# Per-token scales in 128 partitions: a row in DRAM and broadcast loads in place of products with diagonals

## The chip, the cores and the metric

The kernel runs on one core of a Trainium2 chip. The time is the device time of one execution in microseconds, as the median of several runs. PE is the engine for matrix products, DVE the vector engine, ACT the one for activations, POOL is GpSimd; SP issues the DMAs, all of them on one queue here, in the order of the program.

## The reference

One encoder layer, applied to a prompt of 256 tokens and a sample of 2048, width 1024, in float32:

```python
h = rms_norm(x, g_pre)
proj = h @ w_in                     # q, k, v, z_a, u_f, z_f, 512 columns each
y_a = neighbourhood_attention(q, k, v, rpb)
y_f = fourier_mix(u_f, w_fourier, b_fourier)
mixed = concat([rms_norm(y_a, g_na) * silu(z_a), rms_norm(y_f, g_f) * silu(z_f)])
out = mixed @ w_out
return x + rms_norm(out, g_post)
```

`rms_norm` multiplies each token by `rsqrt(mean(x*x) + 1e-6)` and each column by `g`. The change is about the first of these, the token's scale of `h`.

## The kernel before

**Products.** Each product in full precision is three matmuls (`mm3`, L164 to L166) on a high and a low part of both operands. The high part is a cast by ACT, the low part a difference by DVE. For most of the sample the kernel multiplies fewer blocks by forming sums and differences of blocks of `x` and of the weights first.

**Token scales.** `rows_square` sums the squares of rows with tokens on partitions, and `row_scales` makes the scales: column `c` of `invt` (128 x 18) holds those of the 128 tokens of tile `c`. Tiles 0 and 1 are the prompt, 2 to 9 the first half of the sample, 10 to 17 its second half. `row_scales` runs three times: for columns 0 to 3, 4 to 9, and much later 10 to 17.

Where a product has tokens on its output's partitions, the scale is applied afterwards, one number a partition (`vu_out`, L339, into `vo` and `uo`). Where `x` lies with its columns on partitions and tokens along the row, the scales must be a row of numbers that stands in every one of the 128 partitions. Two places need it: `xp` (L721, the prompt, then split into `ph` and `pl`) and `n_scale` (L404, tiles `nx` of the sample, on which the sums and differences are then formed; first half with `x` None, second half with `x` 0 and 1).

Before, such a row is made on PE. `diag` lets ACT multiply the identity by a column of `invt`, which gives a diagonal matrix `dg`; `spread` multiplies a matrix of ones (`onesq`) by it, so that each output partition holds the scales of 128 tokens in order (L309), in PSUM tiles `ivt` (prompt) and `iv` (two of 512 tokens a half). DVE reads them there.

**Order.** All engines follow the order of the program, written out by hand. Ahead of the place come `u` and `v` products for tiles `c` 0 to 2, then a loop over `c` = 3, 4, 5: at `c` = 3 SP issues three loads of `wz`, ACT makes ten diagonals, DVE forms sums `r_sum`; after the products of `c` = 3 PE makes the first ten spreads. At `c` = 4 DVE makes `xp`. Then 16 blocks `b` multiply `ph` and `pl` by weights, split into `wh` and `wl` two blocks ahead (`b_raw`, L566 to L571), while `n_scale` works on `nx` for the first half (`b` < 8). `vu` forms more of `u` and `v`. Then a loop over `i` of 16 and `j` of 7 multiplies the sample by the other weights: at `i` = 0 the last `row_scales` (`j` = 1), eight diagonals (`j` = 2) and eight spreads (`j` = 4) for the second half; `n_scale` for it runs at `i` = 1 and 3. Later come `vu` for the second half, the Fourier stages (`u_load`, tile `ut`), the attention and the output product.

Buffers of the tag `vw` (three of 128 x 1024) are used by `vh` in `vu` and by `ut` later; `iv` in the changed kernel takes them too.

Of the kernel before, what the change touches and what calls it, by code (L numbers as in the profile page):

```python
# [10 lines left out]
F32 = mybir.dt.float32  # L11
F32R = mybir.dt.float32r
AF = mybir.ActivationFunctionType
ALU = mybir.AluOpType
# [4 lines left out]
T = TP + TS  # L19
# [149 lines left out]
def build(tc, A, O):  # L169
    nc = tc.nc  # L170
# [3 lines left out]
    dr = es.enter_context(tc.tile_pool(name="dr", bufs=1, space=DRAM))  # L174
# [10 lines left out]
    vN, uN = [dr.tile([2, 32, 32, 512], F32, name=n) for n in ("vN", "uN")]  # L185
    sD = dr.tile([5, 128, 4, 512], F32, name="sD")
    xD = dr.tile([7, 128, 4, 512], F32, name="xD")
    oD = dr.tile([T, D], F32, name="oD")
    yD = dr.tile([2, 4, 128, T], F32, name="yD")
    woD = dr.tile([2, 2, 4, 128, D], F32, name="woD")  # L190
# [2 lines left out]
    ident = cst.tile([128, 128], F32, name="ident")  # L193
# [7 lines left out]
    invt = cst.tile([128, 18], F32, name="invt")  # L201
# [9 lines left out]
    hp = ph.enter_context(tc.tile_pool(name="hp", bufs=1))  # L211
    st = ph.enter_context(tc.tile_pool(name="st", bufs=2))
    ps = es.enter_context(tc.tile_pool(name="ps", bufs=3, space=PSUM))
# [90 lines left out]
        nc.vector.scalar_tensor_tensor(out=invt[:, c0:c0 + n], in0=t, scalar=1.5, in1=y, op0=ALU.add, op1=ALU.mult)  # L304


    def spread(p, c0, n):
        for x in range(n):
            nc.tensor.matmul(p[:, 128 * x:128 * x + 128], onesq, dg[c0][:, 128 * x:128 * x + 128], start=True, stop=True)  # L309
        dg.pop(c0)  # L310

    def diag(c0, n):
        dg[c0] = et("dg")
        for x in range(n):
            nc.scalar.activation(dg[c0][:, 128 * x:128 * x + 128], ident, AF.Copy, scale=invt[:, c0 + x:c0 + x + 1])

    ivp, dg = {}, {}

    def diag_group(sg):
        for b in range(2):  # L320
            diag(2 + 8 * sg + 4 * b, 4)

    def spread_group(sg):
        ivp[sg] = [ps.tile([128, 512], F32, tag="b", name="iv", bufs=2) for b in range(2)]
        for b in range(2):
            spread(ivp[sg][b], 2 + 8 * sg + 4 * b, 4)

    def p_mm(m, c, kps):
        if (m, c) not in acc:
# [5 lines left out]
    def vu_out(m, c):  # L335
        s, b = PL[c]
        o = st.tile([128, 512], F32, tag="f", name=m + "o", bufs=3)
        x = row_tile(c)
        nc.scalar.activation(o, acc.pop((m, c)), AF.Copy, scale=invt[:, x:x + 1])  # L339
        if s is not None:  # L340
            put_rows(m, 0, b, s, o)
        elif m == "u":
            nc.sync.dma_start(uD[c * 128:c * 128 + 128, :], o)
        else:
            for r in range(4):
                nc.sync.dma_start(vP[c, r, 8 * c:8 * c + 32], o[32 * r:32 * r + 32])
                x = 24 * (1 - c)
                nc.sync.dma_start(vP[1 - c, r, 32 * c:32 * c + 8], o[32 * r + x:32 * r + x + 8])
# [51 lines left out]
    def n_scale(x, kh, b, ks=range(4)):  # L400
        v_ = nq[kh, b] if x is None else nq[x, kh, b]
        for k in ks if x is None else range(2):
            kk = 4 * kh + 2 * (x or 0) + k
            nc.vector.scalar_tensor_tensor(out=v_[:, k], in0=v_[:, k], scalar=gpre[:, kk:kk + 1],  # L404
                                           in1=ivp[int(x is not None)][b], op0=ALU.mult, op1=ALU.mult)

    def n_put(x, j, kh, b):
        nc.sync.dma_start(xD[j, :, 2 * x:2 * x + 2], nq[x, kh, b])
# [75 lines left out]
    def et(name):  # L484
        return st.tile([128, 512], F32, tag="e", name=name, bufs=6)
# [200 lines left out]

    for c in range(3):
        vu_out("u", c)

    def wo_load(x):  # L690
        wor[x] = load((128, D), A["wo"][x // 4, x % 4], "wr")
# [11 lines left out]
    for c in range(3, 6):  # L703
        if c < 5:
            wz_load(3)
            x_split(c + 1)
        if c == 3:
            diag(0, 2)
            diag_group(0)
            for q in range(8):  # L710
                r_sum(q)
        if c == 4:
            n_load((0, 0))
            for x in range(1, 5):
                r_put(x)
            xp = k8(F32, "xp", (128, KC, 256))
            hp_, lp_ = [k8(F32R, "p" + x, (128, KC, 256)) for x in "hl"]
            for k in range(KC):
                for t in range(2):
                    ts = slice(128 * t, 128 * t + 128)  # L720
                    nc.vector.scalar_tensor_tensor(out=xp[:, k, ts], in0=xs[t][:, k], scalar=gpre[:, k:k + 1],  # L721
                                                   in1=ivt[:, ts], op0=ALU.mult, op1=ALU.mult)
            nc.scalar.copy(hp_, xp)
            nc.vector.tensor_tensor(out=lp_, in0=xp, in1=f_(hp_), op=ALU.subtract)
        if c == 5:
            n_load((1, 0))
            b_raw(0)
            b_raw(1)
        p_mm("v", c, range(4))
        vu_out("v", c)  # L730
        p_mm("u", c, range(4))
        if c == 3:
            ivt = ps.tile([128, 256], F32, tag="c", name="ivt", bufs=1)
            spread(ivt, 0, 2)
            spread_group(0)
        vu_out("u", c)


    for b in range(16):
# [11 lines left out]
        if b < 8:  # L751
            x, y = divmod(b, 2)
# [63 lines left out]
    for i in range(16):  # L816
# [48 lines left out]
        for j in range(7):  # L865
            if i in (0, 8):
                if j in (0, 3):
                    w_load(i + 1 + j // 3)
                if i == 0 and j == 0:
                    a_split(0, 6)  # L870
                if i == 0 and j == 1:
                    row_scales(10, 8)
                if i == 0 and j == 2:
                    diag_group(1)
                if i == 0 and j == 4:
                    spread_group(1)
                if j == 2:
                    w_sums(i + 1)
                for x in {3: (0, 1), 4: (2, 3), 5: (4, 5), 6: (6,)}.get(j, ()):
                    a_split(i + 1, x)  # L880
            elif i not in (7, 15):
                if j == 0:
                    w_sums(i + 1)
                a_split(i + 1, j)
                if j == 3 and i < 14 and i != 6:
                    w_load(i + 2)
            elif i == 7:
                if j in (3, 4):
                    op_load(j - 3)
                if j in (5, 6):  # L890
                    op_split(j - 5)
                if j == 5:
                    wo_load(0)
            if sg == 0:
                x, y = divmod(7 * (pr - 1) + j, 14)
                if x in (0, 1):
                    if y == 0:
                        n_load(x)
                    elif 3 <= y < 7:
                        n_scale(x, *divmod(y - 3, 2))  # L900
                    elif 7 <= y < 12:
                        n_diff(x, y - 7)
                if pr == 6 and j in (2, 5):
                    (b_split if j > 2 else b_get)(0)
                if pr == 7 and j:
                    b_get(j)
                    if j > 2:
                        b_split(j - 2)
            if i == 2 and j == 0:
                for t, n in ((gmix, "gmix"), (bfs, "bf"), (dnyq, "dnyq"), (rmask, "rmask"), (csm, "csmask")):  # L910
                    nc.sync.dma_start(t, A[n])
                nc.sync.dma_start(cm, A["cmask"].rearrange("p (b x) -> p b x", b=2))
            if i == 5 or 8 <= i < 15:
                t_step(max(0, i - 7), j)
            for f, d in ((u_load, 0), (u_split, 3), (u_stage1, 5)):
                x = 7 * pr + j - 7 - d
                if sg and 0 <= x < 36 and x % 7 in (0, 2, 4):
                    f(x // 7 * 3 + x % 7 // 2)
            if i == 15 and j in (1, 3, 4, 5):
                if j == 1:  # L920
                    d2 = [load_d(0), load_d(1)]
                else:
                    zgs.append(load_z(j - 3))
            if 9 <= i < 15 and j == 2:
                v_copy(i - 9)
            p = mmt(512)
            aw = aop[i, j]
            bh, bl = bnew[sg, j]
            for k in range(4):
                mm3(nc, p, aw[:, 0, k], aw[:, 1, k], bh[:, k], bl[:, k], k == 0, k == 3)  # L930
            add = lambda o, u: nc.vector.tensor_tensor(out=e_(o), in0=uu[u], in1=p, op=ALU.add)
            if j == 0:
                nc.scalar.copy(e_("u0"), p)
            elif j == 1:
                comb(0, 0, "u0", p)
            elif j == 2:
                add("u2", "u0")
            elif j == 3:
                add("u4", "u2")
            elif j == 4:  # L940
                comb(1, 1, "u4", p)
                add("u3", "u2")
            elif j == 5:
                comb(1, 0, "u3", p, ALU.subtract)
                store(1)
            else:
                comb(0, 1, "u4", p)
                store(0)
# [788 lines left out]
```

## Time and profile before

| | |
|---|---|
| median of 3 runs | 988.64 us (988.61 to 988.85) |
| the profiled execution | 989.52 us, its span 987.4 us |
| PE busy | 970.9 us (98%) |
| DVE, ACT, POOL busy | 703.6, 501.7, 428.3 us |
| DMA | 278.70 MB, mean 282 GB/s |
| products with diagonals (L309) | 36 records on PE, from 51.9 to 174.7 us |
| diagonals (L315) | 18 activations of 386 ns |

A row of a group of instructions has line, engine, operation and tiles (written <- read), count, shortest, median and longest duration in ns, and the first and last start in us. A row of a timeline has start and duration in us, engine, line and tiles, and in brackets the idle time of the engine before it and what ended it; several instructions in a row are merged. A row of waits has who waited for whom, the time in us, how often, and the longest. A row of a window has the stretch, its length, the busy time in it of PE, PE's weight loads, DVE, ACT and POOL, the share of full clock that PE had, the share of time in which the 16 DMA engines were busy, and GB/s.

### The profile page before, as it was taken

Reading aid. Unit: us, or ns where it says so; the run is one execution under the profiler, and the core shown is the slowest. Engines: PE = TensorE matmul, PEld = TensorE weight load, DVE = VectorE, ACT = ScalarE, POOL = GpSimd, SP = SyncE. Lnnn points to the kernel's source line nnn. Section 1 sums busy time; section 2 is a strip of 40 time slices with the busy share of each in tenths; the row PEclk is TensorE's granted clock in tenths of the full one; section 3 lists DMA queues with packets and bytes.
Section 4 is the critical chain, followed back from the end, with each engine's and each line's share of the span. In section 5 each row is a group of like instructions: output and inputs, shape, how many; then the busy total and the mean of one; then the engine's idle time right before and its main releaser. Section 6 shows DMA issues by size and latency. Waiting matters only on the chain.

```text
span 987.4 us, 17038 instructions
## 1 busy us (share of the span) xinstructions
PE 970.9 (98%) x5774; PEld 805.5 (82%) x5774; DVE 703.6 (71%) x1301; ACT 501.7 (51%) x1083; POOL 428.3 (43%) x400
## 2 busy tenths in 40 slices
PE   7999999999999999999999999999999999999997
PEld 6889988888888878878887879778787887888886
DVE  6378987777866777777976446775665665659997
ACT  6836676433224533333344255677666675644443
POOL 3100002464741102755755033566587686534444
PEclk9999999999999999999999999999999999999999
DMA  9899686566839997598989887697768799779993
GB/s 327 303 380 340 190 330 249 173 221 247 308 148 358 347 387 260 218 337 313 322 314 339 294 312 296 218 277 263 247 213 260 261 309 315 224 245 340 344 338 125
DMA packets 147046, 278.70 MB, mean 282 GB/s; under 512 B 14160, under 2 KB 85136, under 8 KB 143568
## 3 DMA queue, kind: packets, MB, share of 16 engines
q1 hardware_dynamic: 146960, 277.62, 79.9%
q8 instruction: 46, 0.75, 0.3%
q14 instruction: 40, 0.33, 0.1%
HBM read 183.19 MB, written 101.71 MB: 289 GB/s over the span
## 4 chain that ended last, share of the span: by engine, by line
PE 48%; DMA 2%; DVE 1%; issue 1%; ACT 0%; POOL 0%; SPq 0%; DVEq 0%; ACTq 0%; POOLq 0%
PE po L1406 19%; PE pv L1476 6%; PE ptb L1460 5%; PE s L1155 4%; PE mm L165 2%; PE mm L164 2%; PE mm L166 2%; PE pab L1000 2%; DMA ut<-uN 1%; PE py L164 1%; PE py L166 1%; PE py L165 1%; DMA tb<-tD 1%; DVE ut L372 0%; PE ppq L1038 0%
## 5 line engine op out<-in xcount | busy, mean ns | idle before, releaser
L164 PE MATMUL mm<-xh,wa 128*128 128x512 f32 x448 | 174.4, 389 | 0.0
L165 PE MATMUL mm<-xl,wa 128*128 128x512 f32 x448 | 174.3, 389 | 0.0
L166 PE MATMUL mm<-xh,wa 128*128 128x512 f32 x448 | 174.3, 389 | 0.0
L536 POOL TENSOR_TENSOR ws<-wr 128x512 f32<-128x512 f32 x16 | 22.5, 1408 | 238.8 <-DMA wr<-wz 223.5
L1189 POOL TENSOR_SCALAR w<-w,m 128x480 f32<-128x480 f32 (+6 forms) x136 | 83.3, 625 | 64.6 <-DVE m L1186 50.6
L165 PEld LDWEIGHTS mm<-xl,wa 128*128 128x128 f32 x448 | 84.1, 188 | 17.5
L166 PEld LDWEIGHTS mm<-xh,wa 128*128 128x128 f32 x448 | 84.1, 188 | 17.5
L164 PEld LDWEIGHTS mm<-xh,wa 128*128 128x128 f32 x448 | 84.1, 188 | 17.5
L1406 PE MATMUL po<-wo,yh 128*128 128x512 f32 x272 | 90.4, 413 | 0.0
L1182 ACT ACTIVATE w<-w,m 128x480 f32<-128x480 f32 (+6 forms) x136 | 79.2, 585 | 15.5 <-DVE m L1177 15.5
L1406 PE MATMUL po<-w,yh 128*128 128x512 f32 x280 | 86.7, 391 | 0.0
L551 DVE TENSOR_TENSOR wa<-wr,wa 128x512 fp32r<-128x512 f32 x60 | 62.3, 1045 | 32.0 <-ACT wa L550 31.9
L1177 DVE CUSTOM_DVE_ANT_1 w<-s,tb 128x360 f32<-128x360 f32 (+5 forms) x124 | 62.5, 541 | 9.1 <-PE s L1155 8.5
L165 PE MATMUL mm<-vl,xh 128*128 128x512 f32 x168 | 65.6, 390 | 0.9 <-DVE vl L482 0.9
L589 POOL TENSOR_TENSOR mt<-mt,rmask 128x880 f32<-128x880 f32 (+2 forms) x24 | 53.7, 2250 | 27.6 <-DMA ut<-uN 15.5
L166 PE MATMUL mm<-vh,xl 128*128 128x512 f32 x168 | 65.4, 389 | 0.0
L164 PE MATMUL mm<-vh,xh 128*128 128x512 f32 x168 | 65.4, 389 | 0.0
L1476 PEld LDWEIGHTS pv<-pt,v 128*64 128x64 f32 (+4 forms) x896 | 47.4, 135 | 19.0 <-issue 14.9
L1476 PE MATMUL pv<-pt,v 128*64 128x128 f32 (+4 forms) x896 | 62.3, 280 | 0.0
L854 DVE TENSOR_TENSOR f<-u,mm 128x512 f32<-128x512 f32 x64 | 43.6, 681 | 25.2 <-PE mm L166 15.4
L1406 PEld LDWEIGHTS po<-w,yh 128*128 128x128 f32 x280 | 52.3, 188 | 10.9 <-issue 0.2
L1460 PE MATMUL ptb<-ident,w 128*128 128x128 f32 (+4 forms) x428 | 59.9, 277 | 0.0
(253 smaller groups left out, 2384.9 us busy)
## 6 DMA issues: line engine op xcount, KB each, us to landing
wr<-wz SPq DMA_DIRECT2D x48, 512.0 KB
vl<-sD SPq DMA_DIRECT2D x20, 512.0 KB
xm<-xm SPq DMA_DIRECT2D x9, 1024.0 KB
oD<-ofs SPq DMA_DIRECT2D x18, 512.0 KB
of<-oD SPq DMA_DIRECT2D x18, 512.0 KB
yr<-yD SPq DMA_DIRECT2D x34, 256.0 KB
zD<-f SPq DMA_DIRECT2D x16, 512.0 KB
woD<-wo SPq DMA_DIRECT2D x16, 512.0 KB
```

The costliest lines, as they stand in the source:

```text
L164: nc.tensor.matmul(out, lh, rh, start=first, stop=False)
L165: nc.tensor.matmul(out, lh, rl, start=False, stop=False)
L166: nc.tensor.matmul(out, ll, rh, start=False, stop=last)
L551: nc.vector.tensor_tensor(out=o[:, 1], in0=src, in1=o[:, 0].bitcast(F32), op=ALU.subtract)
L589: nc.gpsimd.tensor_tensor(out=o, in0=i, in1=rmask[:, m0:m0 + n].unsqueeze(2).to_broadcast([128, n, 80]), op=ALU.add)
L854: nc.vector.tensor_tensor(out=dst(f, b), in0=src(uu[u]), in1=src(p), op=op)
L1177: nc.vector.tensor_tensor_reduce(out=rows(g["w"][b][:, h, :n], w), in0=rows(g["s"][2 * b + h][:, :n], w), in1=tv, scale=1.0, scalar=3.0e38 ...
L1182: nc.scalar.activation(w, w, AF.Exp, bias=m[:, h:h + 1], scale=-1.0, accum_out=m[:, 2 + h:3 + h])
L1189: nc.gpsimd.tensor_scalar(w, w, m[:, 4 + h:5 + h], 1.0, ALU.mult, ALU.mult)
L1406: nc.tensor.matmul(p, (d["l"] if x == 2 else d["h"])[:, c], w(n, int(x == 1), c), start=j == 0, stop=j == 11)
L1460: nc.tensor.transpose(ptb[h][:nk, j * 128:j * 128 + 128], g["w"][b][:, h, c0:c0 + nk], ident)
L1476: nc.tensor.matmul(p[hs, b], g["v"][:nk, v, hs], g["pt"][b][:nk, h, j * 128:j * 128 + 128], start=j == 0, stop=j == len(ch) - 1)
```

## The change

`diag`, `spread` and their groups go. `iv_put` stores columns of `invt` as one row of `ivD` in DRAM, and `iv_get` loads a stretch of that row into all 128 partitions, into an SBUF tile `iv`. The columns 0 to 9 are stored after the `u` outputs of `c` = 2 and loaded at `c` = 3 in two parts (prompt, first half), where the diagonals were made; columns 10 to 17 are stored at `i` = 0, `j` = 3 and loaded at `j` = 5. All of these DMAs are on SP's queue. `xp` and `n_scale` read the SBUF tile.

```diff
+    ivD = dr.tile([1, T], F32, name="ivD")
...
-    def spread(p, c0, n):
-        for x in range(n):
-            nc.tensor.matmul(p[:, 128 * x:128 * x + 128], onesq, dg[c0][:, 128 * x:128 * x + 128], start=True, stop=True)
-        dg.pop(c0)
-
-    def diag(c0, n):
-        dg[c0] = et("dg")
-        for x in range(n):
-            nc.scalar.activation(dg[c0][:, 128 * x:128 * x + 128], ident, AF.Copy, scale=invt[:, c0 + x:c0 + x + 1])
...
+    ivb = {}
+
+    def iv_put(c0, n):
+        nc.sync.dma_start(ivD[0, c0 * 128:(c0 + n) * 128].rearrange("(c p) -> p c", p=128), invt[:, c0:c0 + n])
+
+    def iv_get(c0, n):
+        t = hp.tile([128, 1024], F32, tag="vw", name="iv", bufs=3)
+        nc.sync.dma_start(t[:, :128 * n], ivD[:, c0 * 128:(c0 + n) * 128].to_broadcast([128, 128 * n]))
+        ivb[c0] = t
...
-                                           in1=ivp[int(x is not None)][b], op0=ALU.mult, op1=ALU.mult)
+                                           in1=ivb[2 if x is None else 10][:, 512 * b:512 * b + 512], op0=ALU.mult, op1=ALU.mult)
...
     for c in range(3):
         vu_out("u", c)
+    iv_put(0, 10)
...
         if c == 3:
-            diag(0, 2)
-            diag_group(0)
+            iv_get(0, 2)
+            iv_get(2, 8)
...
-                                                   in1=ivt[:, ts], op0=ALU.mult, op1=ALU.mult)
+                                                   in1=ivb[0][:, ts], op0=ALU.mult, op1=ALU.mult)
...
-        if c == 3:
-            ivt = ps.tile([128, 256], F32, tag="c", name="ivt", bufs=1)
-            spread(ivt, 0, 2)
-            spread_group(0)
...
-                if i == 0 and j == 2:
-                    diag_group(1)
-                if i == 0 and j == 4:
-                    spread_group(1)
+                if i == 0 and j == 3:
+                    iv_put(10, 8)
+                if i == 0 and j == 5:
+                    iv_get(10, 8)
```

More of the change, by code (lines that the diff above doesn't have):

```diff
@@ L304, in row_scales @@
         nc.vector.scalar_tensor_tensor(out=invt[:, c0:c0 + n], in0=t, scalar=1.5, in1=y, op0=ALU.add, op1=ALU.mult)
-    def spread(p, c0, n):
-        for x in range(n):
-            nc.tensor.matmul(p[:, 128 * x:128 * x + 128], onesq, dg[c0][:, 128 * x:128 * x + 128], start=True, stop=True)
-        dg.pop(c0)
-    def diag(c0, n):
-        dg[c0] = et("dg")
-        for x in range(n):
[L315 to L326, printed above, removed]
+    ivb = {}
[5 more added lines that the diff above has]
+        ivb[c0] = t
     def p_mm(m, c, kps):
```

## The prediction, made before the changed kernel ran

> **What bounds the kernel now.** I read the page first, then who waited for whom on PE, then the instructions on the two tiles that the change removes, and last the timelines around them.
>
> ```profile
> PE 970.9 (98%) x5774; PEld 805.5 (82%) x5774; DVE 703.6 (71%) x1301; ACT 501.7 (51%) x1083; POOL 428.3 (43%) x400
> ...
> q1 hardware_dynamic: 146960, 277.62, 79.9%
> ...
> PE 48%; DMA 2%; DVE 1%; issue 1%; ACT 0%; POOL 0%; SPq 0%; DVEq 0%; ACTq 0%; POOLq 0%
> ```
>
> PE is busy for 98% of the span, and where the chain of the work that ended last leaves PE, it does so for a few per cent only. Busy time of pipelined matmuls can flatter, so I checked what PE waited for:
>
> ```profile
> PE mm L164 <- ACT xh L283: 5.4, 1, 5.4
> PE pz L165 <- DVE ut L372: 1.5, 2, 0.9
> PE mm L165 <- DVE vl L482: 0.9, 2, 0.7
> PE mm L166 <- DVE wl L570: 0.6, 3, 0.2
> ```
>
> The first is PE's first wait, at the start of the kernel. All the others together are about 3 us of 987. So an instruction that leaves PE's queue is worth its whole slot, unless a stretch in which something else sets the pace swallows it; and the change can cost time only by making PE wait. These two questions carry the rest.
>
> **What leaves PE.**
>
> ```profile
> L309 PE MATMUL iv<-dg,onesq x32: 270/275/275, 52.4 to 174.7; 128*128 128x128 f32 x32
> L315 ACT ACTIVATE dg<-ident,invt x18: 386/387/402, 48.4 to 171.5; 128x128 f32<-128x128 f32 x18
> ...
> L309 PE MATMUL ivt<-dg,onesq x4: 270/274/275, 51.9 to 52.3; 128*128 128x128 f32 x4
> ```
>
> Eighteen products with a diagonal show as 36 records, two each, in two places: 20 near 52 us and 16 near 173 us. Their durations overlap, so 36 times 275 ns would be far too much. What counts is the start of the next ordinary matmul:
>
> ```profile
> 51.70 0.39 PE L166 MATMUL mm<-wc,xl 128*128 128x512 f32 x1
> 51.93 0.60 PE L309 MATMUL ivt<-dg,onesq 128*128 128x128 f32 x4
> 52.37 1.95 PE L309 MATMUL iv<-dg,onesq 128*128 128x128 f32 x16
> ...
> 54.39 0.40 PE L165 MATMUL mm<-wc,xh 128*128 128x512 f32 x1
> ```
>
> ```profile
> 172.78 0.39 PE L166 MATMUL mm<-xh,wa 128*128 128x512 f32 x1
> 173.01 1.95 PE L309 MATMUL iv<-dg,onesq 128*128 128x128 f32 x16
> ...
> 175.02 0.40 PE L165 MATMUL mm<-xl,wa 128*128 128x512 f32 x1
> ```
>
> From one ordinary matmul to the next is 51.93 - 51.70 = 0.23 us (0.227 over longer rows). From the L166 at 51.70 to the second ordinary one after the products, at 54.39, are 2.69 us, where two pitches are 0.455: 2.24 us go. I take the second because the first is itself stretched. At 173 us: 175.02 - 172.78 = 2.24, less 0.455, is 1.79 us. Sum 4.03 us, 0.112 us a record.
>
> On ACT 18 activations of 0.387 us go. ACT is busy half of the time and no PE wait in this part is on it, so I count nothing for that. No PSUM tile is waited for here either, so the freed banks count nothing.
>
> **What comes in, first place.** One store writes 10 columns of 128 scales as one row, then two loads bring 128 KB and 512 KB into 128 partitions. All are on SP's queue: the store behind the store of `uo` for c=2, the loads behind the next three loads of `wz`. SP stands at the first load until the store has landed; behind it are the stores of `vo` and `uo` for c=3 and three more `wz` loads.
>
> ```profile
> 47.55 0.32 SPq L352 DMA_DIRECT2D uN<-uo  x1
> 47.96 1.34 SPq L231 DMA_DIRECT2D wr<-wz  x3
> ...
> 51.99 0.33 SPq L352 DMA_DIRECT2D vN<-vo  x1
> ...
> 53.34 2.21 SPq L231 DMA_DIRECT2D wr<-wz  x3
> ```
>
> The store goes out at about 47.9 us. The scales are ready by then, since the activations into `uo` read them. No transfer of the trace has 4-byte runs, so its time is unknown. The nearest row for its fixed part is the load of `gpre`, 128 runs of 32 B:
>
> ```profile
> 1.18 0.42 SPq L624 DMA_DIRECT2D gpre<-gpre  x1
> ...
> 4.21 0.72 ACT L253 ACTIVATE wc<-rv,gpre 128x512 fp32r<-128x512 f32 x1 [1.99 <-DMA gpre<-gpre]
> ```
>
> That took 3.0 us from issue to use. The store has 1280 runs, 80 on each of 16 engines, instead of 8: 72 more. Each costs between nothing and a mean packet: 79.9% of 16 x 987.4 us over 146,960 packets is 86 ns, for 1.9 KB. So the store lands between 47.9 + 3.0 = 50.9 and 50.9 + 72 x 0.086 = 57.1 us. I take 52, near the low end, as the runs carry 4 B and not 1.9 KB. SP had nothing to issue from 49.3 to 51.99 anyway, so at 52 the stores behind slip by a microsecond; at 57 they and the `wz` loads slip by about 5.
>
> The loads then take about the 3 us of `gpre`'s from issue to use, the second behind the first. So the scales of the prompt are there at 55, at worst at 60.1. Who needs them, and when?
>
> ```profile
> 59.85 4.21 DVE L721 SCALAR_TENSOR_TENSOR xp<-xr,gpre,ivt 128x128 f32<-128x128 f32 x16
> ...
> 68.25 2.35 DVE L567 TENSOR_TENSOR wl<-wr,wh 128x1024 fp32r<-128x1024 f32 x2
> 77.84 1.23 DVE L567 TENSOR_TENSOR wl<-wr,wh 128x1024 fp32r<-128x1024 f32 x1 [7.23 <-ACT wh L566]
> ```
>
> ```profile
> 75.93 0.28 PE L164 MATMUL mm<-ph,wh 128*128 128x256 f32 x1
> ```
>
> DVE comes to `xp` at 59.85 because it is busy until then, and the first `wl` behind it ends at about 69.4 (68.25 and half of 2.35), 9.6 us after `xp` begins. PE needs both at 75.93, after the change at 73.7. So `xp` may begin as late as 64.1 before PE waits: even the worst store leaves 4 us. After that DVE stood for 7.23 us, released by ACT and behind it PE, so that stretch moves forward with PE.
>
> The 0.64 MB come while the DMA engines are full (below), at about 400 GB/s, so what is queued behind lands 1.6 us later: inside the slack just worked out, and DVE's idle 7 us.
>
> ```profile
> 50.00:52.00 2.00, 2.00 (x11) 1.65 (x10) 2.00 (x3) 1.96 (x6) 0.00 (x0) 1.00 1.01 387
> ```
>
> **Second place.** The scales are made at 169.2 and first read at 192.5:
>
> ```profile
> 169.20 0.17 DVE L304 SCALAR_TENSOR_TENSOR invt<-rt,ry 128x8 f32<-128x8 f32 x1
> ...
> 192.53 1.40 DVE L404 SCALAR_TENSOR_TENSOR nx<-nx,gpre,iv 128x512 f32<-128x512 f32 x2
> ```
>
> ```profile
> 167.24 1.79 SPq L231 DMA_DIRECT2D wr<-wz  x4
> 183.54 3.63 SPq L860 DMA_DIRECT2D zD<-f  x2
> ```
>
> ```profile
> 175.00:180.00 5.00, 5.00 (x23) 4.13 (x22) 3.76 (x5) 2.25 (x4) 3.88 (x3) 1.00 0.00 0
> ```
>
> The store queues behind four `wz` loads that are through by 175 (the DMA engines then stand still), lands by about 177, at worst 6.2 us later, 183, and the load is there 3 us after it, at 186. SP has nothing to issue until 183.54. `n_scale` comes 1.79 us earlier than before against all this, at 190.7, so nothing is late; a store 4.7 us slower than my worst would make DVE wait.
>
> **DVE's operand.** `xp` and `n_scale` read the scales from SBUF instead of PSUM. The same operation with all operands in SBUF, L254, took as long:
>
> ```profile
> L404 DVE SCALAR_TENSOR_TENSOR nx<-nx,gpre,iv x32: 732/742/746, 79.0 to 242.7; 128x512 f32<-128x512 f32 x32
> ```
>
> ```profile
> L254 DVE SCALAR_TENSOR_TENSOR wc<-rv,gpre,wc x8: 745/751/753, 5.0 to 15.8; 128x512 fp32r<-128x512 f32 x8
> ```
>
> Nothing for that; where GpSimd works beside it, after 192 us, it may be slower, on an engine that is not the bound there.
>
> **Sum.** 2.24 + 1.79 = 4.03 us, costs 0. The profiled execution took 989.52 us, its span 987.4 and 2.1 around it; it would become 985.5. It lies 0.9 over the median of the runs, 988.64, so the runs should show 988.64 - 4.03 = 984.6 us.
>
> **Rivals.** *The store's 4-byte runs are slow, and the kernel becomes slower.* Place: `xp` at 59.85, by way of SP standing behind the store. PE begins to wait when the store lands after 61 us, 13.2 us after its issue, so at (13.2 - 3.0) / 72 = 142 ns a run; it has lost the 4.03 us at 198 ns. At 250 ns the store takes 3.0 + 18.0 = 21.0 us, 7.8 beyond the start of the waiting, and the time is 988.64 - 4.03 + 7.8 = 992.4 (the second place adds a wait of DVE, which I leave out). For it: all 1280 runs go into the same 5 KB of DRAM, from all engines at once, and no row has such a store. Against it: it takes three times the mean packet for a five-hundredth of its bytes.
>
> The Trainium skill's "DMA: Bandwidth & Descriptors" speaks for this rival in "Rules for kernel authors" (a strided last dimension becomes one descriptor per element) and in "Specifications" (transfers under 512 B are done as read-modify-write); its "Latency and other measured facts" gives 0.2 us for one access to HBM. If every run paid that in turn, an estimate from that page is 3.0 + 72 x 0.2 = 17.4 us, 988.8 us in all, where the gain is just gone. No run so far shows it.
>
> *The gain is swallowed later.* PE waits for `vl` near 355 us and for `ut` near 427 and 525, both fed by DMAs, in stretches in which the DMA engines are full (PE's busy time of the 5 us, then, at the end of the row, the DMA engines' share):
>
> ```profile
> 355.00:360.00 5.00, 4.60 (x20) 3.83 (x21) 4.58 (x6) 2.72 (x3) 0.00 (x0) 1.00 1.02 410
> 425.00:430.00 5.00, 4.09 (x19) 3.02 (x18) 4.80 (x5) 2.84 (x6) 4.87 (x3) 1.00 0.97 329
> ```
>
> If these run at the DMA's pace whatever PE does, PE comes 4 us early and waits 4 us more: 988.6. Half swallowed, 986.6. Against it: both stretches begin with an empty DMA queue,
>
> ```profile
> 290.00:295.00 5.00, 5.00 (x24) 4.14 (x23) 3.57 (x5) 0.00 (x0) 0.00 (x0) 1.00 0.00 0
> 335.00:340.00 5.00, 5.00 (x23) 4.14 (x23) 4.32 (x6) 3.29 (x4) 0.00 (x0) 1.00 1.02 401
> ...
> 405.00:410.00 5.00, 5.00 (x24) 4.14 (x23) 5.00 (x5) 0.21 (x2) 5.00 (x3) 1.00 0.00 0
> ```
>
> filled again by issues that wait for buffers and results, so they come 4 us earlier too.
>
> *The store is moderately slow* (142 to 198 ns): part of the gain is lost, 985 to 988.6.
>
> **Chances.** The full gain, within a microsecond: 0.62. Swallowed in part or whole: 0.14, half of it still faster. Moderate store: 0.08, half of it still faster. Slow store, or a wait of its kind that I don't see: 0.16. A measurement of this kernel tells 0.2% from no change, 2.0 us: faster means under 986.7. That makes faster 0.73, same 0.11, slower 0.16. The range goes from 983.3 (the gain, and besides it the longest wait for `vl`, 0.7, and the shorter of the two for `ut`, 0.6) to 988.8, where all of the gain is gone.
>
> **What would show it.** Right: PE has 36 records fewer, and the ordinary matmuls run through 52 and 173 us with a pitch of 0.227; the loads of `iv` land by 60; DVE still begins `xp` near 59.85 or earlier; PE's waits for `vl`, `ut` and `wl` stay at about 3 us. Wrong in the first way: DVE's idle time before `xp` is put down to the DMA of `iv`, and PE waits at the first matmul with `ph`. Wrong in the second: no wait near 60, but longer waits at 355 to 525. SP's time on the store, far over the 0.3 to 0.4 us of other issues, would be a cost that I have not counted.

## The result and the profile after

The changed kernel took 995.87 us in the median of four runs (993.72 to 997.47), the kernel before 988.75 on the same chip (988.61 to 989.26): 1.007 times as long, 95% interval 1.005 to 1.009. Forecast were 984.6 us, range 983.3 to 988.8. The profiled execution is the shortest of the four, 993.72 us, with a span of 991.9; nothing here explains what the other three have on top of it. Four executions far outside the rest (1210 us in `e13_unread_64`, 1942 in `e6_late_sums`, 5476 in `e5_none`, 5499 in the kernel before beside the last two) are left out of the figures below.

Line numbers shift: in the changed kernel `iv_put` is L311, `iv_get` L315, `vo` and `uo` L329, their stores L342, `n_scale` L394, `wh` L556, `wl` L557, `xp` L712. First the page's line of busy times, and who waited for whom on PE in the whole span (us in total, times, longest):

```profile
PE 969.1 (98%) x5738; PEld 803.1 (81%) x5738; DVE 712.1 (72%) x1301; ACT 495.2 (50%) x1065; POOL 429.6 (43%) x400
```

```profile
PE mm L164 <- ACT wh L556: 5.8, 2, 5.4
PE mm L164 <- ACT xh L284: 5.2, 1, 5.2
PE pz L165 <- DVE ut L362: 1.4, 2, 0.8
PE mm L166 <- DVE wl L557: 1.2, 2, 0.8
```

PE has 5738 records, 36 fewer, as forecast. But 7.0 us of waits for `wh` and `wl` are new. The timelines of SP, DVE, ACT and PE around that place show the chain:

```profile
46.90 0.38 SPq L311 DMA_DIRECT2D ivD<-invt  x1
47.38 1.67 SPq L232 DMA_DIRECT2D wr<-wz  x3
58.64 1.01 SPq L315 DMA_DIRECT2D iv<-ivD  x2
...
71.58 0.32 SPq L342 DMA_DIRECT2D vN<-vo  x1
```

```profile
50.53 0.39 PE L166 MATMUL mm<-wc,xl 128*128 128x512 f32 x1
...
64.74 4.29 DVE L712 SCALAR_TENSOR_TENSOR xp<-xr,gpre,iv 128x128 f32<-128x128 f32 x16 [5.86 <-DMA iv<-ivD]
...
73.91 0.69 ACT L329 ACTIVATE vo<-mm,invt 128x512 f32<-128x512 f32 x1
83.94 0.69 ACT L329 ACTIVATE uo<-mm,invt 128x512 f32<-128x512 f32 x1 [9.34 <-DMA vN<-vo]
84.53 1.03 ACT L556 CAST wh<-wr 128x1024 fp32r<-128x1024 f32 x1
...
73.12 0.38 PE L164 MATMUL mm<-ph,wh 128*128 128x256 f32 x1 [0.44 <-ACT wh L556]
74.49 0.39 PE L166 MATMUL mm<-ph,wl 128*128 128x256 f32 x1 [0.75 <-DVE wl L557]
...
85.62 0.58 PE L164 MATMUL mm<-ph,wh 128*128 128x256 f32 x1 [5.36 <-ACT wh L556]
```

The store goes out at 46.90 and the load behind it at 58.64, when the store has landed: 11.7 us. `xp` waits 5.86 us for `iv` and starts at 64.74, 4.9 us later than before; PE is idle for 0.44 + 0.75 us by that. The large wait stands twelve microseconds on. ACT cannot write `uo` of `c` = 5, because the output buffers (three of them) are still being read by the store of `vo` of `c` = 4, issued at 71.58 behind 4 MB of stores of the sums. `wh` for the next block stands behind `uo` on ACT, and PE behind `wh`: 5.36 us.

A second cost follows the wait. The windows from 84 to 94 us (busy time of PE, PE's weight loads, DVE, ACT, POOL, then clock, DMA share, GB/s):

```profile
84.00:86.00 2.00, 0.38 (x2) 0.39 (x2) 0.40 (x1) 1.98 (x3) 0.00 (x0) 0.58 0.98 396
86.00:88.00 2.00, 1.54 (x7) 1.24 (x7) 2.00 (x3) 1.99 (x3) 0.00 (x0) 0.50 1.12 347
88.00:90.00 2.00, 2.00 (x11) 2.00 (x11) 1.92 (x3) 1.41 (x3) 0.00 (x0) 0.50 0.97 371
90.00:92.00 2.00, 2.00 (x15) 2.00 (x14) 2.00 (x4) 0.27 (x1) 0.00 (x0) 0.71 0.95 339
92.00:94.00 2.00, 2.00 (x19) 2.00 (x19) 2.00 (x3) 2.00 (x3) 0.00 (x0) 1.00 1.03 405
```

After 5.4 us without work the granted clock is 0.50 until about 91 us. The matmuls from 85.62 to 91.10 took 5.48 us; the same ones took 2.52 in the kernel before. 0.46 of the difference is a wait, so some 2.5 us are lost to the clock. The Trainium skill's "TensorE: Matmul & The Clock Gate" has this in "What's actually happening": half clock after an idle window of about 3.4 us, full clock again after about 3.4 us of sustained work. The half clock agrees with the rows, the figures do not: the way back took some 5.5 us here, and in `e3_rows` below a wait of 2.29 us was enough.

Idle times do not give the whole cost, since matmuls overlap; the starts of the same matmul in both kernels do (here and below, the times that go with such a comparison are those of the kernel before). The last one ahead of the place starts at 50.53 us here and at 51.70 before: this execution is 1.17 us ahead before it meets anything that the change touches. (It gets there between 6 and 15 us. `e6_late_sums`, the same program up to there, is 0.02 ahead, so that differs from one execution to the next.) Behind the removed products PE is 3.42 us ahead, 2.25 of it saved. The late scales take 1.8 of that by 77 us, the large wait and the half clock another 8.5: with 0.1 later on, 10.4 us are lost in this place. The next stage begins with a wait for `vl` in both kernels, first before, then after:

```profile
124.14 0.50 PE L165 MATMUL mm<-vl,xh 128*128 128x512 f32 x1 [0.21 <-DVE vl L482]
```

```profile
131.16 0.50 PE L165 MATMUL mm<-vl,xh 128*128 128x512 f32 x1 [0.21 <-DVE vl L472]
```

PE is 7.0 us late here. The second place gives 1.8 back, about 1 comes back near 355, where the wait for `vl` (0.7) is gone, and the end is 4.5 us late (991.9 against 987.4), 5.7 without the early start.

**Where the store spent its time.** Summaries of the DMAs: the changed kernel from 48 to 50 us and from 49 to 58 us, then the kernel before from 49 to 58 us:

```profile
DMA packets 1344, 0.08 MB, mean 42 GB/s; under 512 B 1312, under 2 KB 1312, under 8 KB 1344
```

```profile
DMA packets 66, 0.27 MB, mean 30 GB/s; under 512 B 1, under 2 KB 1, under 8 KB 66
```

```profile
DMA packets 951, 2.92 MB, mean 324 GB/s; under 512 B 108, under 2 KB 108, under 8 KB 950
```

All but one of the small packets have passed by 49 us. In the nine after that only 66 packets pass, where the kernel before moved 951, though three loads of `wz` of 512 KB are issued and waiting. The store is through as packets, hasn't landed, and what is queued behind it crawls. At the second place (182 to 189 us) there is nothing behind it, and the DMA engines stand still until it lands:

```profile
176.75 0.40 SPq L311 DMA_DIRECT2D ivD<-invt  x1
189.19 0.33 SPq L315 DMA_DIRECT2D iv<-ivD  x1
```

```profile
DMA packets 277, 0.00 MB, mean 0 GB/s; under 512 B 277, under 2 KB 277, under 8 KB 277
```

12.4 us there, of which some 5 go by behind four loads of `wz`.

### The profile page after: what moved, and what is told of

Its sections match the earlier page's. It is cut to its first block, busy times and chain, and to the rows that moved or that the text cites. A ratio compares the mean times of both kernels' runs of the same rounds, so it can differ in the third digit from the quotient of the medians.

```text
span 991.9 us, 16955 instructions
## 1 busy us (share of the span) xinstructions
PE 969.1 (98%) x5738; PEld 803.1 (81%) x5738; DVE 712.1 (72%) x1301; ACT 495.2 (50%) x1065; POOL 429.6 (43%) x400
## 4 chain that ended last, share of the span: by engine, by line
PE 50%; DVE 1%; issue 1%; POOL 0%; DMA 0%; SPq 0%; DVEq 0%; ACT 0%; POOLq 0%
PE po L1393 19%; PE pv L1463 6%; PE ptb L1447 5%; PE s L1142 4%; PE mm L165 3%; PE mm L164 3%; PE mm L166 3%; PE pab L987 2%; PE py L164 1%; PE py L166 1%; PE py L165 1%; PE ppq L1025 0%; PE ppq L1032 0%; PE pna L1437 0%; PE pfn L1430 0%
## 5 line engine op out<-in xcount | busy, mean ns | idle before, releaser
L166 PEld LDWEIGHTS mm<-xh,wa 128*128 128x128 f32 x448 | 84.1, 188 | 17.4
L1451 DVE COPY pt<-ptb 128x384 f32<-128x384 f32 (+2 forms) x72 | 41.1, 571 | 25.5 <-PE ptb L1447 24.8
```

What stands on the lines that cost most here:

```text
L166: nc.tensor.matmul(out, ll, rh, start=False, stop=last)
L1451: V.tensor_copy(o[:, h, :n], ptb[h][:, :n])
```

## Experiments

Theories: the harm is the store in the first place, by making SP stand (S), or by holding up the DMA engines for everybody (D); the removed products are worth their 4.03 us, or less.

**One place at a time.** `e1_first_only` keeps diagonals and products of the second place, `e2_second_only` those of the first (shown is one line of `n_scale`, against the kernel before):

```diff
...
-  in1=ivp[int(x is not None)][b]
+  in1=ivb[2][:, 512 * b:512 * b + 512] if x is None else ivp[1][b]      # e1
+  in1=ivp[0][b] if x is None else ivb[10][:, 512 * b:512 * b + 512]      # e2
```

> Only the first place (prompt and first half of the sample) goes through DRAM; the second half keeps its eight products with diagonals. My theory: all of the loss is in the first place, where PE has 2.24 us less to do, waits 7.0 us (0.44, 0.75, 5.36 and 0.46 in the profile of the changed kernel) and loses about 2.5 us at half clock behind the longest wait. So 988.7 - 2.2 + 9.5 = 996, give or take 2. Rival, that the second place costs as well (its store took 12.4 us too): then this kernel is clearly faster than the changed one, 990 to 992.

> Only the second place goes through DRAM; prompt and first half keep their products with diagonals. My theory: SP had nothing else to issue there and n_scale comes late enough, so PE keeps the whole 1.79 us: 986.9. Rival, the second place costs as well: 989 to 993, with PE waits near 190 to 250 us.

Measured: first place alone 1000.46 us (ratio to before 1.0116, 1.0099 to 1.0133), second alone 989.40 (1.0003, 0.9993 to 1.0013). All of the harm comes with the first place, but both sizes were missed. `e1` is 4.6 us slower than the changed kernel, above the 994 to 998 that I gave: it lacks the 1.8 us of the second place, and in its profile PE loses another 4.7 us from 425 to 431 us, to two waits for `ut` (1.7 and 0.8 us) and a half clock behind them. The second place was to give 986.9 and is worth nothing by time, though PE has no new wait near it: PE's waits between 300 and 540 us, first before, then second place alone:

```profile
PE pz L165 <- DVE ut L372: 1.5, 2, 0.9
PE mm L165 <- DVE vl L482: 0.7, 1, 0.7
```

```profile
PE pz L165 <- DVE ut L383: 2.5, 6, 0.8
PE pz L164 <- ACT ut L382: 0.3, 1, 0.3
PE pz L165 <- DMA ut<-uN: 0.2, 1, 0.2
```

Three waits became eight, 2.2 us became 3.0. By the starts of the same matmuls PE gains 1.8 us at 175 and 0.8 near 355, and loses 3.1 from 425 to 526: the whole gain is given back in the Fourier stage, which waits for `ut`.

**The store with long runs.** `e3_rows` turns the ten columns into ten rows on PE and stores runs of 512 B; `e4_unread` is the same with the change's store added, to an array that nobody reads:

```diff
 def iv_put(c0, n):
-    nc.sync.dma_start(ivD[...].rearrange("(c p) -> p c", p=128), invt[:, c0:c0 + n])
+    nc.tensor.transpose(p[:n], invt[:, c0:c0 + n], ident)
+    nc.scalar.copy(t[:n], p[:n])
+    nc.sync.dma_start(ivD[...].rearrange("(c p) -> c p", p=128), t[:n])
...
+nc.sync.dma_start(ixD[0, :1280].rearrange("(c p) -> p c", p=128), invt[:, :10])   # e4 only
```

> Both places, but the columns of scales are first turned into rows on PE (one transpose of 128 x 10, one of 128 x 8) and copied by ACT, so that the store writes 10 (or 8) runs of 512 B in place of 1280 (1024) of 4 B; the store for the first place follows the v products of c = 3, and the loads follow it at once. My theory, that the 4-byte runs are the whole cost: the stores land in 2 to 3 us, xp starts at its old time, PE saves 4.03 us less two short transposes (0.2 to 0.5 us): 984.8 to 985.3. Rival, that the detour through DRAM costs as such (a wait of SP and 1.2 MB more in a stretch in which the DMA engines are full): 988 or more, with waits of PE near 75 us.

> As the kernel with rows, and beside it the old store of 1280 runs of 4 B, at its old place in SP's queue, into an array that nobody reads: nobody waits for it. Theory S, the cost is that SP stands until the store has landed: then this kernel is as fast as the one with rows, about 985. Theory D, the writes to DRAM hold up the DMA engines themselves, so that the transfers behind them crawl whether SP waits or not (66 packets from 49 to 58 us in the changed kernel, with 1.5 MB outstanding): then the loads of the scales land late here too, 60 us or later, and the time is 992 to 996.

Measured: `e3_rows` 991.33 us (1.0024, 1.0011 to 1.0037), `e4_unread` 1000.87 (1.0122, 1.0105 to 1.0139). A store for which nobody waits costs 9.5 us: theory S, that only the wait for this store costs, falls; theory D holds in kind, at more than its 992 to 996. The DMAs of `e4_unread` from 49 to 58 us:

```profile
DMA packets 615, 0.26 MB, mean 28 GB/s; under 512 B 553, under 2 KB 553, under 8 KB 615
```

SP stands here all the same, at the load of the rows, whose own store of ten runs now lands late:

```profile
50.03 0.60 SPq L316 DMA_DIRECT2D ivD<-ivs  x1
64.74 0.79 SPq L320 DMA_DIRECT2D iv<-ivD  x2
```

14.7 us from issue to landing, against 5.6 in `e3_rows`. What the held-up DMAs would cost if SP stood nowhere was not tested.

`e3_rows` missed its 984.8 to 985.3 too; its rival, 988 or more, came. `xp` was on time (59.87) and PE waited for `wh` all the same, 2.29 us. Its timelines of ACT and PE, and a window behind the wait:

```profile
79.38 0.69 ACT L333 ACTIVATE uo<-mm,invt 128x512 f32<-128x512 f32 x1 [9.65 <-DMA vN<-vo]
...
81.06 0.58 PE L164 MATMUL mm<-ph,wh 128*128 128x256 f32 x1 [2.29 <-ACT wh L560]
...
82.00:84.00 2.00, 1.69 (x8) 1.69 (x9) 1.92 (x4) 1.99 (x5) 0.00 (x0) 0.50 0.95 296
```

SP stood 5 us at the load there too, everything behind came closer together, and the store of `vo` lay behind those of the sums. The half clock followed this shorter wait as well; by the starts of the same matmuls the two together cost some 6 us.

**What the products are worth.** In `e5_none` the scales in the partitions are tiles of ones: no store, no load, no product.

```diff
...
-  nc.sync.dma_start(t[:, :128 * n], ivD[:, c0 * 128:(c0 + n) * 128].to_broadcast([128, 128 * n]))
+  nc.gpsimd.memset(t[:, :128 * n], 1.0)
```

> The changed kernel without its DRAM detour and without the products: the scales that xp and n_scale read are tiles of ones, written once by GpSimd, so this part of the computation is left out. It gives the worth of the 36 records by themselves. Theory W, as in my prediction: PE is the bound, so they are worth their whole 4.03 us: 984.7. Theory P, some stretches are paced by DMA: the activation into uo for c = 5 waits for a buffer whose store lands near 75 us whatever PE does (it was read at 76.18 before, and would come at 73.9), and the loads of ut set the pace from 424 to 526 us, so of 4.03 us only about 1 is left: 987.5 to 988.5.

Measured: ratio 0.9976 (0.9964 to 0.9989), 2.4 us of 989.7, between theory W (4.03) and theory P (about 1); in its profile the span is 3.2 us shorter, 984.2. Two rows of its PE timeline, in the kernel before at 427.32 and 476.06:

```profile
423.01 0.50 PE L165 MATMUL pz<-ut,f1h 128*128 128x512 f32 x1 [0.86 <-DVE ut L358]
473.51 0.50 PE L165 MATMUL pz<-ut,f1h 128*128 128x512 f32 x1 [0.47 <-DVE ut L358]
```

PE is 4.3 us early at the first and 2.5 at the second, 0.87 of it from the start of the execution. By the starts of the same matmuls it gains 2.25 us at 52 and 1.80 at 173, so the 4.03 us do leave PE. It loses 0.8 at a wait for `wl` near 97, gains 0.6 near 355, loses 2.0 at `ut` from 425 to 476 and gains 0.6 there at 525: 2.3 us are left, and with the 0.87 the 3.2 of the profile.

**Orders that give the store more room.** `e6_late_sums` is the changed kernel with the stores of the sums (`sD`, 1 MB each) put off to blocks 0 to 3. `e7_rows_early` is `e3_rows` with the transpose and store right after the first `u` output, loads ahead of `wz`. `e9_rows_early_late_sums` has both.

```diff
-            for x in range(1, 5):       # c == 4: e6, e9
-                r_put(x)
...
+        if b < 4:
+            r_put(b + 1)
...
+        if c == 0:                      # e7, e9
+            p_mm("v", 3, range(2))
+            iv_put(0, 10)
+            p_mm("v", 3, range(2, 4))
+    iv_get(0, 2)
+    iv_get(2, 8)
...
```

> The changed kernel with one edit: four stores of the sums (4 MB) are issued one in each of the blocks b = 0 to 3, not all at c = 4, so that the store of vo for c = 4 no longer lies behind them. Theory P: the 5.36 us wait of PE near 85 us, and the 2.5 us at half clock behind it, come from that store and its buffer; they go, and the time is 987 to 991. Rival, that the wait comes from the late scales alone (xp at 64.7): unchanged, 995 to 997.

> As the kernel with rows, with the first store moved ahead: the transpose stands in the middle of the v products of c = 3, the copy and the store behind the first uo, and the two loads ahead of the next wz loads. SP then waits a microsecond at most and the DMA engines never run empty, so what is left over the products is 0.64 MB of loads (1.6 us of a full DMA queue) and two transposes. Theory W: 985.0. Theory P: PE still waits 1 to 2.5 us near 78 to 81 us, and the time is 987.5 to 989.5.

> The two edits together: rows, stored early, and the stores of the sums issued later. Theory P: no PE wait near 80 us any more, so the 2.24 us of the first place are kept; those of the second are swallowed at the ut loads: 986 to 987.5. Theory W: 985.0, no faster than the kernel with rows stored early alone.

Measured: `e6` 992.42 to 995.45 us (1.0049, 1.0023 to 1.0074), `e7` 989.70 (1.0001, 0.9990 to 1.0012), `e9` 992.31 (1.0029, 1.0018 to 1.0040). In `e6` the 5.4 us near 85 are gone, but the DMA queue is as full as before, and now `f` waits for the store of an earlier `f`; PE's waits from 60 to 130 us:

```profile
PE mm L164 <- ACT wh L556: 2.4, 1, 2.4
PE mm L166 <- DVE wl L557: 1.2, 2, 0.6
```

The half clock follows this 2.4 us wait too: by the starts of the same matmuls `e6` loses 6.1 us between 95 and 110. I had expected 987 to 991 of `e6` and a gain of `e9` over `e7`: both misses. The late sums move the jam and don't clear it. `e7`, for which I had 985.0 or 987.5 to 989.5, is the best form with a detour through DRAM, and it takes as long as the kernel before.

**The store by itself.** Three kernels before, each with a chain of probe stores near 280 to 327 us where the DMA engines otherwise stand still; a load behind each store waits for it, so SP's issues give the landings. Their own times (1009.30, 1014.33, 1022.70 us) contain the probes and say nothing of the change.

```diff
+            if i == 6 and j == 3:
+                probe()
...
+  nc.sync.dma_start(pD[0, :].rearrange("(c p) -> p c", p=128), invt[:, :10])              # side by side
+  nc.sync.dma_start(pS[:, 0:1].rearrange("(c p) w -> p c w", p=128), ...unsqueeze(2))      # pS is 1280 x 16: 64 B apart
```

> The kernel before, with a chain of probe transfers near 280 to 300 us, where the DMA engines otherwise stand still: each store is followed on SP's queue by a load of what it wrote, so SP's waits give each landing. In order: a store of 128 runs of 40 B; the change's 1280 runs of 4 B transposed into 5 KB; half of them (640); 1280 runs of 4 B that lie 64 B apart in DRAM; 1280 that lie 512 B apart; a load of 1280 runs of 4 B; a store of 40 B runs. Theory M (the writes of 4 B pass one by one through one place of the DRAM, about 7.4 ns each): issue to landing some 2 us, 11.5, 7, then 3 to 5 for each of the two spread stores, because they meet in other places; Theory N (every run of 4 B costs the same wherever it lies): 2, 11.5, 7, 11.5, 11.5. Theory P (the cost is the packets' own, not the writes'): the load of 4 B runs takes about 11.5 too; by M and N it takes 3 to 4. If none of the stores of 4 B takes over 5 us here, the 11.7 us of the change came from the other traffic around it.

SP's timeline, each store followed by the load that waits for it:

```profile
286.08 0.43 SPq L613 DMA_DIRECT2D pD<-invt  x1
296.47 0.29 SPq L615 DMA_DIRECT2D pbb<-pD  x1
296.81 0.38 SPq L616 DMA_DIRECT2D pH<-invt  x1
306.68 0.26 SPq L618 DMA_DIRECT2D pbc<-pH  x1
306.99 0.36 SPq L619 DMA_DIRECT2D pS<-invt  x1
309.83 0.23 SPq L621 DMA_DIRECT2D pbd<-pS  x1
310.11 0.36 SPq L622 DMA_DIRECT2D pW<-invt  x1
313.07 0.23 SPq L624 DMA_DIRECT2D pbe<-pW  x1
```

The DMAs of the same trace from 288 to 296 us:

```profile
DMA packets 0, 0.00 MB, mean 0 GB/s; under 512 B 0, under 2 KB 0, under 8 KB 0
```

1280 runs side by side: 10.4 us with nothing else on the queue, of which eight pass without a packet. 640: 9.9, so theory M (7.4 ns a run) falls. The same 1280 runs 64 B apart 2.8 us, 512 B apart 3.0: theories N and P fall. Loading 1280 such runs took 2.3 us, storing 128 runs of 40 B 1.4. The number of runs isn't what costs, nor that they are short; it matters how close together they lie in DRAM.

> A second chain of probe stores near 280 to 320 us, each followed by a load of its first element, so that SP's waits give each landing. The first chain had 10.4 us for 1280 runs of 4 B side by side, 9.9 for 640, 2.9 when they lie 64 B or 512 B apart. In order here: 1280 runs side by side; 16 runs in one stretch of 64 B; 128 runs in 512 B; 1280 runs 8 B apart (8 to a stretch of 64 B), 16 B apart (4), 32 B apart (2); 128 runs 64 B apart. Theory L (writes into the same stretch of 64 B follow one another, the first in 2.4 to 2.9 us, each further one (10.4 - 2.9) / 15 = 0.5 us, and different stretches pass side by side): 10.4; 9.5 to 10 for the mere 16 runs; 10; 6.4; 4.4; 3.4; 2.5. Theory M (all writes of 4 B pass one place, 7.4 ns each) is all but fallen with the 640 runs: 11.5; 2.5; 3.4; 11.5 and so on. Theory B (a larger block, 512 B, is the unit): 10 for the 128 runs, 2.5 to 4 for the 16, and the pitches of 8 to 32 B fall less than in proportion.

From issue of the store to issue of the load, by SP's timeline (the first store, queued behind other loads, 14.2 us): 1280 runs 8 B apart 6.2 us, 16 B 4.1, 32 B 3.2, 128 runs side by side 7.8, 64 B apart 1.4. Theory L had 6.4, 4.4, 3.4, 10 and 2.5. SP's waits for the 128 runs side by side and for the 16, which begin after the issue of the store:

```profile
SPq L616 <- DMA pC<-invt: 7.4, 1, 7.4
...
SPq L616 <- DMA pL<-invt: 1.0, 1, 1.0
```

The pitches go as forecast, about 0.45 us for each further write into the same 64 B. The last row does not: 16 runs in one stretch of 64 B took 1.3 us, not 9.5. Theory B gives these 16 better, but not the pitches: over the 2.8 us at 64 B the cost is 7.6, 3.4, 1.3 and 0.4 us at 4, 8, 16 and 32 B, so it falls by more than half each time, where B had it fall by less.

> A third chain of probe stores at the same place, each followed by a load of its first element. The second chain gave, from issue of the store to issue of the load: 7.8 us for 128 runs of 4 B side by side, 1.4 for 128 runs 64 B apart, 6.2, 4.1, 3.2 for 1280 runs 8, 16, 32 B apart (so about 0.45 us for each further write into the same 64 B), but 1.3 for 16 runs side by side, where that rule said 7 to 8. In order here: 128 runs side by side (the first one queues behind other loads); 1280 runs 8 B apart in the order of the change; 1280 runs 8 B apart with the ten of one partition next to each other; 32 runs side by side; 64 runs side by side; 16 runs from every eighth partition, side by side; 128 side by side again. Theory W (the writes wait for one another only where they come from several of the DMA engines; the 16 runs went by one): second 6.2, third near 3, since a partition's runs go by one engine; 32 and 64 between 1.4 and 7.8 by the number of engines they go by. Theory L (any further write into the same 64 B costs its 0.45 us, and the 16 runs were a special case of a very small transfer): third 6.2 like the second; 64 runs 7.8, 32 runs 7.8 or 1.4; 16 runs from other partitions 1.3.

Measured: 1280 runs 8 B apart in the order of the change 5.1 us, with one partition's ten next to each other 9.2; 32 runs side by side 3.2, 64 runs 6.6, 16 runs from every eighth partition 2.6, 128 again 7.9. Theory W has the pair at 8 B the wrong way round and falls; theory L doesn't give the 9.2, nor the 16, 32 and 64. Crowding is the cause: the same runs further apart are cheap. It isn't a matter of the spacing alone, as the pair at 8 B shows, and the cost rises from 1.3 or 2.6 us for 16 runs side by side to 7.8 for 128, but only to 10.4 for 1280. Which writes wait for which isn't settled.

**Back in its place.** `e13_unread_64` is `e4_unread` with the unread store's runs 64 B apart.

```diff
-    ixD = dr.tile([1, T], F32, name="ixD")
+    ixD = dr.tile([1280, 16], F32, name="ixD")
...
-    nc.sync.dma_start(ixD[0, :1280].rearrange("(c p) -> p c", p=128), invt[:, :10])
+    nc.sync.dma_start(ixD[:, 0:1].rearrange("(c p) w -> p c w", p=128), invt[:, :10].unsqueeze(2))
```

> The kernel of the scales stored as rows, with the extra store of 1280 runs of 4 B that nobody reads, as before, but with its runs 64 B apart in DRAM instead of side by side. Same packets, same bytes, same queue, same place. Side by side it cost 9.5 us (1000.87 against 991.33). If what costs time is that many writes of 4 B go into the same stretch of DRAM, which the probes measured apart from other traffic (10.4 us side by side, 2.9 at 64 B), the store is now worth its packets, 1 us of a full DMA queue, at most the 2.9 us: 991 to 994. If the cost comes from 1280 small packets in a full queue, it stays at 999 to 1002.

Measured: 991.60, 993.32 and 996.83 us; ratio 1.0065 (1.0040 to 1.0091). Its DMAs from 49 to 58 us:

```profile
DMA packets 1915, 1.88 MB, mean 208 GB/s; under 512 B 1385, under 2 KB 1395, under 8 KB 1914
```

1.88 MB pass where 0.26 did, and the store of the rows lands 7.1 us after its issue, where 14.7 were needed beside the crowded store and 5.6 without a second one. In the shortest run nothing of the 9.5 us is left, in the longest 5.5; the three spread too widely for one number, but all lie under the 999.29 to 1001.99 of `e4_unread`.

## Why the prediction was wrong

**What leaves PE: right as a slot, too large as a gain.** The ordinary matmuls run through 52 and 173 us at 0.227 us, and in `e5_none` PE gains 2.25 + 1.80 us there, against 2.24 + 1.79. Only 2.4 us reach the time. The rival "The gain is swallowed later" named the main place (`ut`, though not the wait for `wl` near 97), and half is about what it took; I gave it 0.14.

**The store: mis-sized, and the model was wrong.** I took 52 for the landing, 57.1 at worst, 3 us and 72 runs an engine at up to 86 ns. It landed by 58.6, 11.7 us after its issue at 46.9; 10.4 us with nothing else on the queue. The packets took their 1 to 2 us, as the low end had it; the rest is after the packets, where no count of packets sees it. The slow-store rival had the right sign for the store, at the wrong size (it began to wait at 13.2 us) and by a price a run, which 640 against 1280 runs rules out. The Trainium skill's "DMA: Bandwidth & Descriptors" warns of one descriptor per element in "Rules for kernel authors" and of transfers under 512 B in "Specifications". That agrees in sign, but neither gives the price: 64 B apart the same 1280 runs of 4 B took 2.8 us. The estimate from its 0.2 us an access, 17.4 us, was too high.

**"The loads then take about the 3 us of `gpre`'s": 6.1.** From its issue at 58.64 to `xp` at 64.74, in a queue with 1.5 MB of `wz` held up in front of it. `xp` was to be able to begin as late as 64.1, and with PE 1.17 us ahead only until 62.9; it began at 64.74. That is 1.8 us too late, and 1.8 us is what it cost PE.

**"What is queued behind lands 1.6 us later": the step that cost most.** I counted the bytes of the loads, not that the store holds other transfers to a tenth of their bytes for nine microseconds (0.27 MB against 2.92), and of DVE's 7.23 us before the third `wl` I wrote "that stretch moves forward with PE". It was put down to ACT's `wh`; one step further back, on ACT, `uo` of `c` = 5 needs a buffer that the store of `vo` of `c` = 4 frees. Before, PE was later than that store and ACT waited for PE; its row in the timeline of the kernel before:

```profile
76.18 0.69 ACT L339 ACTIVATE uo<-mm,invt 128x512 f32<-128x512 f32 x1 [4.80 <-PE mm L166]
```

After, `uo` waited 9.34 us for that store. In `e5_none`, with no new transfer at all, it waited 4.9 us for it and started at 74.69, 1.5 us earlier than before: PE being earlier was enough to turn the releaser round. `e3_rows` shows that path costing some 6 us with `xp` on time, `e6_late_sums` that the wait goes when the stores of the sums no longer lie ahead of that store. The forecast put the costs of this place at nothing; they were 10.4 us.

**Second place, DVE's operand: right in effect.** The store took 12.4 us, but PE and DVE came late themselves, and the scales were never waited for. In `e2_second_only`, where nothing ahead is late, it landed at 184.75, past my worst of 183, and they weren't waited for either; but `n_scale` began 2.3 us later than before, as it waited for a load of `nx` that SP issued behind the store. PE had no new wait before 426 us. `n_scale` takes 747 ns against 742. The instructions on `iv`:

```profile
L394 DVE SCALAR_TENSOR_TENSOR nx<-nx,gpre,iv x32: 740/747/1776, 86.7 to 252.5; 128x512 f32<-128x512 f32 x32
```

Of the signs, the one for "Wrong in the first way" came: DVE's idle time put down to the DMA of `iv`, and PE waiting at the first matmul with `ph`. The one for SP did not: issuing the store took 0.38 us as other issues do, and SP stood at the load behind it. The 5.36 us of PE at 85 stood under none.

## What to carry to other kernels

A transfer's price is not only its own landing: ask what it does to everything queued behind it, and follow each idle time back until a buffer or a transfer stands at its root, since a releaser named "ACT" can be a store one step further. Columns turned into a row by a store of 4 B runs side by side are worth avoiding where the queue is in use; make the rows first and store long runs. And count what a wait costs PE by the starts of the same matmul in both kernels, after taking off what the execution was ahead or behind before the change: waits of 2.3 to 5.4 us each cost 2 to 3 us more than they show. A gain on the bounding engine is worth its slot only as far as the next stage that a transfer paces: running the kernel with the work simply left out gives the ceiling before anything is built.

## What I had not expected of the hardware

1280 stores of 4 B side by side, 5 KB in all, took 10.4 us from issue to landing, 8 of them after their packets had passed; 64 B apart 2.8 us. While they drained, loads from other arrays came through at about 30 GB/s, where the kernel before moved 324. A wait of 5.4 us on PE cost another 2.5 us at half clock, and waits of 2.3 to 2.4 us (`e3_rows`, `e4_unread`, `e6_late_sums`) were followed by half clock as well, while one of 1.45 (`e1_first_only`) and those of 0.75 were not.
